# FFN-down of a decoder layer: squares of two token tiles, two k-tiles and two column chunks, 24 of 64 in a seven-product form

## The chip, the core and the metric

One NeuronCore of a Trainium2 chip runs the whole program in one launch. The metric is the device time of one execution in microseconds (us), lower is better; before the change it is 1213.66 us, the median of three runs (1212.97, 1213.66, 1217.4).

## The reference, cut to what matters

One decoder layer over 256 tokens of width 2048, in float32: a token mixer, then the MLP (the part that changes), then a gated per-layer embedding and a final norm.

```python
h2 = rms_norm(x, mlp_norm[i])
x = x + jnp.square(jax.nn.relu(h2 @ w_ffn_up[i])) @ w_ffn_down[i]   # 2048 -> 8192 -> 2048

gate = jax.nn.sigmoid(rms_norm(x, ple_norm[i]) @ w_ple_gate[i])     # 2048 -> 2048
x = x + gate * (p[i] @ w_ple_proj[i])                               # 256 -> 2048
```

## The kernel before

**Split operands.** TensorE multiplies in fp32r, a shortened float32. To keep float32 accuracy every operand is stored twice: h is the value rounded to fp32r, l is the rest (value minus h). Each product is then three matmuls into one PSUM bank: `a_h w_h`, `a_h w_l`, `a_l w_h` (lines 174 to 176). Weights come from HBM as panels of 256 rows by 512 columns, in SBUF a tile of 128 x 1024 float32 (two k-tiles side by side, 512 KB). `load_raw` (L141) issues the DMA from SP's queue, `split_w` (L146) makes `wh` by two 512-wide copies on ScalarE (ACT, L152) and `wl` by one 1024-wide subtraction on VectorE (DVE, L153). The three tiles raw, wh and wl each rotate over 3 buffers (pool `wp`). A buffer is written again only when its last reader is through.

**MLP.** The hidden width of 8192 is worked in two halves (`ffn_half`, L1068). In each, 8 calls of `gemm_wide` (L990) compute 512 hidden columns each; after every half of a call `square` (L1074) squares the positive part of two k-tiles of hidden activations (128 hidden columns by 256 tokens each) and splits them with `split_sb` (L156) into a tile y, which stays in SBUF as the stationary operand of FFN-down. Then `gemm_toks` (L195) runs FFN-down for four chunks n of 512 output columns. For each chunk it goes through 16 panels, each with two k-tiles and two token tiles, and accumulates into two of four PSUM banks (tag mm): 16 x 2 x 2 x 3 = 192 matmuls of 128 x 512 a chunk, 768 a half, 1536 in all. At a chunk's end `scaled_residual` (L1097) adds the two banks to the residual stream x (tiles xr) on VectorE. In the second half, `h3_part` (L1018) follows each chunk: 8 transposes of x on TensorE into a wide PSUM bank (pool psw, two of two banks), copied out by ScalarE (L1031) and VectorE (L1032). They are the operand of the gate product.

**After the MLP.** The projection of p (four short `gemm_toks`, tile pp), then the gate product in chunks: chunks 0 to 2 by `gemm_toks`, chunk 3 from weights that `keep` (L1057) had split earlier into tiles gk: four during the last chunk of FFN-down (hooks at panels 5, 8, 11, 14), two in each of the first two gate chunks. The last chunk is computed token tile by token tile, so that the end of the program is short.

**What sets the order.** Inside the program a scheduler orders the instructions of each engine; weights' splits and some residual additions carry a high priority. Each engine works through its own queue in order, and an instruction that waits holds back all behind it. Up to the end of the token mixer TensorE's order is the written one (L306).

## Time and profile before

| what | value |
|---|---|
| runs | 1212.97, 1213.66, 1217.4 us (median 1213.66) |
| profiled execution | span 1216.2 us; the profile gives no time outside the span, and the span stands 2.5 us above the median and inside the range of the runs |
| TensorE (PE), busy | 1198.4 us, 99% of the span |
| weight loads (PEld), busy | 1028.3 us, 85% |
| VectorE (DVE), busy | 742.8 us, 61% |
| ScalarE (ACT), busy | 640.1 us, 53% |
| DMA | 216.88 MB, mean 178 GB/s |
| granted TensorE clock, mean | 0.996 |

How to read it: a group's row gives the line, the engine, the operation, the tiles written and read (buffer numbers left out), shapes and count, then the busy time in us and the mean duration of one in ns, then the idle time of that engine just before and what ended it. A row of a timeline gives the start, the duration, and the instruction; the distance between two starts need not be the duration of the first, since an engine can begin an instruction before the one ahead has ended. A row of stretches gives the stretch, its length and for each engine the busy time and the number of instructions, then the granted clock, the share of the DMA engines and GB/s. DMA rows give the time from issue to landing.

### The profile page before, as it was taken

How to read it: one execution, taken by the hardware profiler on the slowest of the kernel's cores; microseconds unless marked ns; L12 is line 12 of the kernel's file. 1: busy time of each engine (PE TensorE's matmuls, PEld its weight loads, DVE VectorE, ACT ScalarE, POOL GpSimd, SP SyncE). 2: the span in 40 equal slices, each digit the busy share in tenths (PEclk: the TensorE clock that was granted, in tenths of full speed). 3: DMA queues.
4: the chain of work that ended last, by engine and by line, in shares of the span. 5: the costliest groups of instructions: out<-in, count | busy, mean ns of one | idle time of the engine just before them, and what ended most of it. 6: DMA issues, size and time to landing. Idle time of an engine off the chain costs nothing.

```text
span 1216.2 us, 18355 instructions
## 1 busy us (share of the span) xinstructions
PE 1198.4 (99%) x7142; PEld 1028.3 (85%) x7142; DVE 742.8 (61%) x938; ACT 640.1 (53%) x1175; POOL 15.4 (1%) x65
## 2 busy tenths in 40 slices
...
GB/s 272 124 198 116 168 152 102 108 185 139 133 238 177 180 188 182 187 189 188 193 190 192 192 197 193 182 187 190 188 182 187 192 187 190 193 255 224 200 123 70
DMA packets 60616, 216.88 MB, mean 178 GB/s; under 512 B 6769, under 2 KB 7537, under 8 KB 60145
## 3 DMA queue, kind: packets, MB, share of 16 engines
...
q10 hardware_dynamic: 288, 0.51, 0.1%
...
HBM read 213.59 MB, written 2.10 MB: 177 GB/s over the span
## 4 chain that ended last, share of the span: by engine, by line
PE 93%; DVE 3%; DMA 1%; ACT 1%; issue 1%; ACTq 0%; DVEq 0%
PE u_w L1004 20%; PE u_w L1008 10%; PE d_b L174 9%; PE d_b L175 9%; PE d_b L176 9%; PE gt_b L175 2%; PE gt_b L176 2%; PE gt_b L174 2%; PE wag_b L335 1%; PE zp_b L174 1%; PE zv_b L165 1%; PE zp_b L176 1%; PE zp_b L175 1%; PE zv_b L166 1%; PE zv_b L167 1%; PE o_b L174 1%
## 5 line engine op out<-in xcount | busy, mean ns | idle before, releaser
L1004 PE MATMUL u_w<-h,wh_u 128*128 128x512 f32 x1024 | 362.1, 399 | 0.0
L1008 PE MATMUL u_w<-h,wl_u 128*128 128x256 f32 x1024 | 287.8, 281 | 0.0
L153 DVE TENSOR_TENSOR wl_d<-raw_d,wh_d 128x1024 fp32r<-128x1024 f32 x128 | 156.9, 1225 | 166.8 <-ACT wh_d L152 166.8
L153 DVE TENSOR_TENSOR wl_u<-raw_u,wh_u 128x1024 fp32r<-128x1024 f32 x128 | 156.8, 1225 | 142.2 <-ACT wh_u L152 142.2
L152 ACT ACTIVATE wh_d<-raw_d 128x512 fp32r<-128x512 f32 x256 | 147.5, 624 | 182.0 <-PE d_b L176 161.0
L152 ACT ACTIVATE wh_u<-raw_u 128x512 fp32r<-128x512 f32 x256 | 147.6, 624 | 179.6 <-PE u_w L1004 89.6
L1004 PEld LDWEIGHTS u_w<-h,wh_u 128*128 128x128 f32 x1024 | 192.5, 188 | 47.9
L176 PE MATMUL d_b<-wh_d,y 128*128 128x512 f32 x512 | 199.8, 390 | 0.0
L174 PE MATMUL d_b<-wh_d,y 128*128 128x512 f32 x512 | 199.7, 390 | 0.0
L175 PE MATMUL d_b<-wl_d,y 128*128 128x512 f32 x512 | 199.6, 390 | 0.0
L1008 PEld LDWEIGHTS u_w<-h,wl_u 128*128 128x128 f32 x1024 | 193.7, 189 | 0.0
L176 PEld LDWEIGHTS d_b<-wh_d,y 128*128 128x128 f32 x512 | 96.1, 188 | 19.9
L174 PEld LDWEIGHTS d_b<-wh_d,y 128*128 128x128 f32 x512 | 96.2, 188 | 19.9
L175 PEld LDWEIGHTS d_b<-wl_d,y 128*128 128x128 f32 x512 | 96.2, 188 | 19.6
L153 DVE TENSOR_TENSOR wl_gt<-raw_gt,wh_gt 128x1024 fp32r<-128x1024 f32 x24 | 29.4, 1224 | 24.4 <-ACT wh_gt L152 24.4
L152 ACT ACTIVATE wh_gt<-raw_gt 128x512 fp32r<-128x512 f32 x48 | 27.7, 625 | 23.3 <-PE gt_b L176 19.3
L165 PE MATMUL zv_b<-hTh,wh_zv 128*128 128x256 f32 x128 | 37.7, 294 | 0.0
L165 PE MATMUL zr_b<-hTh,wh_zr 128*128 128x256 f32 x128 | 37.5, 293 | 0.0
L174 PE MATMUL gt_b<-wh_gt,h 128*128 128x512 f32 x96 | 37.4, 389 | 0.0
L175 PE MATMUL gt_b<-wl_gt,h 128*128 128x512 f32 x96 | 37.4, 389 | 0.0
L176 PE MATMUL gt_b<-wh_gt,h 128*128 128x512 f32 x96 | 37.4, 389 | 0.0
L167 PE MATMUL zr_b<-hTh,wl_zr 128*128 128x256 f32 x128 | 37.1, 290 | 0.1
...
## 6 DMA issues: line engine op xcount, KB each, us to landing
raw_u<-in_w_ffn_up_dram SPq DMA_DIRECT2D x128, 512.0 KB, 3.5
raw_d<-in_w_ffn_down_dram SPq DMA_DIRECT2D x128, 512.0 KB, 3.5
...
```

Source lines behind the costliest of these rows:

```text
L152: nc.scalar.activation(wh[:, a * 512 : (a + 1) * 512], raw[:, a * 512 : (a + 1) * 512], AF.Copy)
L153: nc.vector.tensor_tensor(wl, raw, wh.bitcast(F32), op=ALU.subtract)
L165: nc.tensor.matmul(o, w_h, ah, start=first and ct % 2 == 0, stop=False, skip_group_check=True)
L166: nc.tensor.matmul(o, w_h, al, start=False, stop=False, skip_group_check=True)
L167: nc.tensor.matmul(o, w_l, ah, start=False, stop=last, skip_group_check=True)
L174: nc.tensor.matmul(o, a_h, wh[:, 0:n], start=first, stop=False)
L175: nc.tensor.matmul(o, a_h, wl[:, 0:n], start=False, stop=False)
L176: nc.tensor.matmul(o, a_l, wh[:, 0:n], start=False, stop=last)
L335: nc.tensor.matmul(wag_banks[tt][:, 0:288], xg[k // 4][:, k % 4, tt * 128 : (tt + 1) * 128], wr[k], start=k == 0, stop=k == NK - 1,)
L1004: nc.tensor.matmul(bank[:, ct, :].rearrange("p (s t) -> p s t", s=2), wh[:, c], hl, start=k == 0, stop=False, skip_group_check=True,)
L1008: nc.tensor.matmul(bank[:, ct, 0:T], wl[:, c], hl[:, 0, :], start=False, stop=k == 15, skip_group_check=True)
```

## The change

Two chunks of columns are worked together. A `sweep` covers one pair of chunks in one half: 16 squares i, each of two token tiles by two k-tiles by two chunks, hence 8 block products. 10 of the 16 squares (plain) do them as before, 24 matmuls, into four PSUM banks p2, p3, p4 and d22. Squares 2, 4, 7, 9, 11 and 13 (`SEVEN`) use Strassen's form in Winograd's variant: seven products of sums of blocks, 21 matmuls, into p1, p6, p5 and p7 (the two wide banks) and p2, p3 and p4. After square 13 the wide banks are added up on VectorE and into the four blocks of x; after square 15 the other four banks follow. There are four sweeps.

For a seven-product square the activations' sums are made once per half, in `square_seven`: four VectorE operations 128 wide, then seven blocks are split in three pieces instead of one. The weights' sums are made in every sweep by `weights_seven`: two raw panels, four 512-wide VectorE differences (tiles t, float32), their splits th and tl (1024 wide, two tiles each, both used up by one square), and the splits w7h and w7l of three plain blocks.

Around it: raw, wh and wl rotate over 4 buffers instead of 3 once the MLP's pool is open (`ring`); constants of the token mixer move to a pool `mc` that closes with it; the h3 transposes stand behind the projections of p instead of behind the chunks of FFN-down; `keep` is called three, three and two times in gate chunks 0, 1 and 2, loads through `load_raw`, and stores in other tiles; scratch tiles change names (junk and t, ph and u).

```diff
+    mc = rctx.enter_context(tc.tile_pool(name="mc", bufs=1))
...
+    extra = []
+    turns = {"raw": 0, "wh": 0, "wl": 0}
+
+    def ring(tag, dt, name):
+
+        if extra:
+            turns[tag] += 1
+            if turns[tag] % 4 == 0:
+                return extra[0].tile([128, 1024], dt, tag=f"{tag}x", name=name)
+        return wp.tile([128, 1024], dt, tag=tag, name=name)
+
     def load_raw(src, n, name):
-        raw = wp.tile([128, 1024], F32, tag="raw", name=f"raw_{name}")
+        raw = ring("raw", F32, f"raw_{name}")
         nc.sync.dma_start(raw[:, 0:n], src)
         return raw
 
     def split_w(raw, name):
 
-        wh = wp.tile([128, 1024], F32R, tag="wh", name=f"wh_{name}")
-        wl = wp.tile([128, 1024], F32R, tag="wl", name=f"wl_{name}")
+        wh, wl = ring("wh", F32R, f"wh_{name}"), ring("wl", F32R, f"wl_{name}")
...
+    extra.append(fp)
...
+    keep_at = ["yd"] * 5 + ["a5", "ys", "th"]
...
+        where = keep_at[kp]
+        raw = load_raw(w_gate[3, kp].rearrange("p a n -> p (a n)"), 1024, f"gk{kp}")
+        if where == "a5":
+            w = a8(5, f"gk{kp}", F32R)
+            wh, wl = w[:, 0:1024], w[:, 1024:2048]
+        else:
+            bufs = {"yd": 10, "ys": 2, "th": 2}[where]
+            wh, wl = (fp.tile([128, 1024], F32R, tag=where, bufs=bufs, name=f"gk{kp}{c}") for c in "hl")
...
+    SEVEN = (2, 4, 7, 9, 11, 13)
+    F_A11, F_A12, F_A22, F_S1, F_S3, F_S2, F_S4 = range(7)
+    def mm(o, l, r, first, last):
+        nc.tensor.matmul(o, l, r, start=first, stop=last, skip_group_check=True)
+    def mm3(o, a, w, first, last):
+        (a_h, a_l), (w_h, w_l) = a, w
+        mm(o, a_h, w_h, first, False)
+        mm(o, a_h, w_l, False, False)
+        mm(o, a_l, w_h, False, last)
+    def square_plain(src, pr):
+        d = fp.tile([128, 1024], F32R, tag="yd", bufs=10, name=f"yd{pr}")
+        split_sb(d[:, 0:512], d[:, 512:1024], src)
+        def block(i, j):
+            o = j * T + i * 128
+            return d[:, o : o + 128], d[:, 512 + o : 512 + o + 128]
+        return block
+    def square_seven(src, pr, q):
+        if q < 4:
+            y = a8((0, 1, 2, 5)[q], f"ys{pr}", F32R)[:, 0:1792]
+        else:
+            y = fp.tile([128, 1792], F32R, tag="ys", bufs=2, name=f"ys{pr}")
+        yh, yl = (y[:, c : c + 896].rearrange("p (f t) -> p f t", t=128) for c in (0, 896))
+        k1t0, k1t1, k2t0, k2t1 = (src[:, c * 128 : (c + 1) * 128] for c in range(4))
+        sf = fp.tile([128, 4, 128], F32, tag="u", bufs=3, name=f"sf{pr}")
+        nc.vector.tensor_tensor(sf[:, 0], k1t1, k2t1, op=ALU.add)
+        nc.vector.tensor_tensor(sf[:, 1], k1t0, k1t1, op=ALU.subtract)
+        nc.vector.tensor_tensor(sf[:, 2], sf[:, 0], k1t0, op=ALU.subtract)
+        nc.vector.tensor_tensor(sf[:, 3], k2t0, sf[:, 2], op=ALU.subtract)
+        tok0 = src.rearrange("p (k t) -> p k t", k=2)[:, :, 0:128]
+        split_sb(yh[:, 0:2], yl[:, 0:2], tok0)
+        split_sb(yh[:, 2], yl[:, 2], k2t1)
+        split_sb(yh[:, 3:7], yl[:, 3:7], sf)
+        return lambda f: (yh[:, f], yl[:, f])
+    def weights_seven(ra, rb, name):
+        b11, b21, b12, b22 = ra[:, 0:512], ra[:, 512:1024], rb[:, 0:512], rb[:, 512:1024]
+        t = [fp.tile([128, 1024], F32, tag="t", bufs=2, name=f"t{i}_{name}") for i in range(2)]
+        th = [fp.tile([128, 1024], F32R, tag="th", bufs=2, name=f"th{i}_{name}") for i in range(2)]
+        tl = [fp.tile([128, 1024], F32R, tag="tl", bufs=2, name=f"tl{i}_{name}") for i in range(2)]
+        ha, hb = (ring("wh", F32R, f"w7h{i}_{name}") for i in range(2))
+        la, lb = (ring("wl", F32R, f"w7l{i}_{name}") for i in range(2))
+        with tc.high_priority(20000):
+            nc.scalar.activation(ha, ra, AF.Copy)
+            nc.vector.tensor_tensor(la, ra, ha.bitcast(F32), op=ALU.subtract)
+            nc.vector.tensor_tensor(t[0][:, 0:512], b12, b11, op=ALU.subtract)
+            nc.vector.tensor_tensor(t[0][:, 512:1024], b22, b12, op=ALU.subtract)
+            nc.scalar.activation(hb[:, 512:1024], b22, AF.Copy)
+            nc.vector.tensor_tensor(lb[:, 512:1024], b22, hb[:, 512:1024].bitcast(F32), op=ALU.subtract)
+            nc.scalar.activation(th[0], t[0], AF.Copy)
+            nc.vector.tensor_tensor(t[1][:, 0:512], b22, t[0][:, 0:512], op=ALU.subtract)
+            nc.vector.tensor_tensor(t[1][:, 512:1024], b21, t[1][:, 0:512], op=ALU.subtract)
+            nc.vector.tensor_tensor(tl[0], t[0], th[0].bitcast(F32), op=ALU.subtract)
+            nc.scalar.activation(th[1], t[1], AF.Copy)
+            nc.vector.tensor_tensor(tl[1], t[1], th[1].bitcast(F32), op=ALU.subtract)
...
+        return {
+            "b11": half(ha, la, 0), "b21": half(ha, la, 1), "b22": half(hb, lb, 1),
+            "t1": half(th[0], tl[0], 0), "t3": half(th[0], tl[0], 1),
+            "t2": half(th[1], tl[1], 0), "t4": half(th[1], tl[1], 1),
+        }
+    def sweep(src, acts, np_, name, residual_, hooks=()):
+        hooks = dict(hooks)
+        p2, p3, p4, d22 = (mm_bank(f"{name}_{q}") for q in ("p2", "p3", "p4", "d22"))
+        w1, w2 = wide_bank(f"{name}_w1"), wide_bank(f"{name}_w2")
+        p1, p6, p5, p7 = w1[:, 0], w1[:, 1], w2[:, 0], w2[:, 1]
+        n0, n1 = 2 * np_, 2 * np_ + 1
+        begun = set()
+        last_seven = max(SEVEN)
+        npair = len(acts)
+        def put(which, o, a, w, last):
+            mm3(o, a, w, which not in begun, last)
+            begun.add(which)
+        for i in range(npair):
+            if i in hooks:
+                hooks[i]()
+            ra, rb = (load_raw(src[n, i].rearrange("p a n -> p (a n)"), 1024, f"{name}_{n}_{i}") for n in (n0, n1))
+            if i in SEVEN:
+                w = weights_seven(ra, rb, f"{name}_{i}")
+                a = acts[i]
+                fin = i == last_seven
+                for which, o, f, t, last in (
+                    ("p1", p1, F_A11, "b11", fin), ("p2", p2, F_A12, "b21", False), ("p3", p3, F_S4, "b22", False),
+                    ("p5", p5, F_S1, "t1", fin), ("p7", p7, F_S3, "t3", fin), ("p6", p6, F_S2, "t2", fin),
+                    ("p4", p4, F_A22, "t4", False),
+                ):
+                    put(which, o, a(f), w[t], last)
+                if fin:
+                    u = [fp.tile([128, 512], F32, tag="u", bufs=3, name=f"u{c}_{name}") for c in range(3)]
+                    nc.scalar.activation(u[0], p1, AF.Copy)
+                    nc.vector.tensor_tensor(u[1], p6, u[0], op=ALU.add)
+                    residual_(n0, 0, u[0])
+                    nc.vector.tensor_tensor(u[2], p7, u[1], op=ALU.add)
+                    nc.vector.tensor_tensor(u[1], p5, u[1], op=ALU.add)
+                    residual_(n1, 0, u[1])
+                    residual_(n0, 1, u[2])
+                    nc.vector.tensor_tensor(u[2], p5, u[2], op=ALU.add)
+                    residual_(n1, 1, u[2])
+            else:
+                ws = [split_w(r, f"{name}_{n}_{i}") for n, r in ((n0, ra), (n1, rb))]
+                end = i == npair - 1
+                for which, o, tt, b in (("p2", p2, 0, 0), ("p3", p3, 0, 1), ("p4", p4, 1, 0), ("d22", d22, 1, 1)):
+                    for j in range(2):
+                        put(which, o, acts[i](tt, j), ws[b][j], end and j == 1)
+                    if end:
+                        residual_((n0, n1)[b], tt, o)
+    def scaled_residual(n, tt, src):
+        xs = xr[tt][:, n * 512 : (n + 1) * 512]
+        with tc.high_priority(30000):
+            nc.vector.scalar_tensor_tensor(xs, src, s2[:, tt : tt + 1], xs, op0=ALU.mult, op1=ALU.add)
...
-                split_sb(y[:, bi * 512 : bi * 512 + 512], y[:, 1024 + bi * 512 : 1024 + bi * 512 + 512], r)
+                pr = i * 2 + bi
+                if pr in SEVEN:
+                    acts.append(square_seven(r, f"{hf}_{pr}", SEVEN.index(pr)))
+                else:
+                    acts.append(square_plain(r, f"{hf}_{pr}"))
             gemm_wide(w_up[f], h2, f"u{f}", square)
-            ys.append(y)
             if f == 1:
                 inv_ms()
-        if hf == 1:
-            h3_part, h3 = transposed("h3")
-            h3_box.append(h3)
...
-            run(gemm_toks(w_down[n, hf * 16 : hf * 16 + 16], act, f"d{hf}_{n}", scaled_residual, None, ahead if (hf, n) == (1, 3) else ()))
-            if hf == 1:
-                h3_part("ple_norm", n)
-    ahead = {kp: keep for kp in (5, 8, 11, 14)}
+        for np_ in range(2):
+            sweep(w_down[:, hf * 16 : hf * 16 + 16], acts, np_, f"d{hf}{np_}", scaled_residual)
     ffn_half(0)
     ffn_half(1)
-    h3 = h3_box[0]
+    h3_part, h3 = transposed("h3")
...
+        h3_part("ple_norm", n)
...
-        run(gemm_toks(w_gate[n], h3, f"gt{n}", gated_both(n), None, {kp: keep for kp in ((1, 4) if n < 2 else ())}))
+        run(gemm_toks(w_gate[n], h3, f"gt{n}", gated_both(n), None, {kp: keep for kp in ((1, 3, 5) if n < 2 else (1, 3))}))
```

How the instructions stand. **TensorE, first sweep.** Before, chunk 0 of the first half, the third panel: d_0_b are the two accumulators (5812 and 5813 the token tiles), wh_d and wl_d the panel's halves, y the activations.

```order
L174 MATMUL d_0_b_5812<-wh_d_0_2_5854,y_4406 128x512
L175 MATMUL d_0_b_5812<-wl_d_0_2_5855,y_4406 128x512
L176 MATMUL d_0_b_5812<-wh_d_0_2_5854,y_4406 128x512
L174 MATMUL d_0_b_5813<-wh_d_0_2_5854,y_4406 128x512
L175 MATMUL d_0_b_5813<-wl_d_0_2_5855,y_4406 128x512
L176 MATMUL d_0_b_5813<-wh_d_0_2_5854,y_4406 128x512
```

Now, the end of square 1 (plain, d_d is d22) and the first three products of square 2: w7h and w7l are the split plain blocks, d_w a wide bank (p1), d_p p2 and p3, ys the seven activation blocks.

```order
L1085 MATMUL d_d_5881<-wh_d_1_1_5931,yd_1_4408 128x512
L1085 MATMUL d_w_5882<-w7h_d_2_5970,ys_2_4508 128x512
L1085 MATMUL d_w_5882<-w7l_d_2_5972,ys_2_4508 128x512
L1085 MATMUL d_w_5882<-w7h_d_2_5970,ys_2_4508 128x512
L1085 MATMUL d_p_5878<-w7h_d_2_5970,ys_2_4508 128x512
L1085 MATMUL d_p_5878<-w7l_d_2_5972,ys_2_4508 128x512
L1085 MATMUL d_p_5878<-w7h_d_2_5970,ys_2_4508 128x512
L1085 MATMUL d_p_5879<-w7h_d_2_5971,ys_2_4508 128x512
L1085 MATMUL d_p_5879<-w7l_d_2_5973,ys_2_4508 128x512
L1085 MATMUL d_p_5879<-w7h_d_2_5971,ys_2_4508 128x512
```

Four accumulators in place of two change every three or six matmuls, and a square of 24 becomes one of 21; products 4 to 7, on th and tl, follow these.

**VectorE, the same half.** Before, the splits of chunk 0's panels stand one after another, with one square() between them:

```order
L153 TENSOR_TENSOR wl_d_0_2_5855<-raw_d_0_2_5852,wh_d_0_2_5854 128x1024
L1078 TENSOR_TENSOR r_1_5806<-u_w_5713,r_1_5806 128x512
L1079 SCALAR_TENSOR_TENSOR r_1_5806<-r_1_5806 128x512
L153 TENSOR_TENSOR wl_d_0_3_5874<-raw_d_0_3_5871,wh_d_0_3_5873 128x1024
L158 TENSOR_TENSOR y_5613<-r_1_5806,y_5613 128x512
L153 TENSOR_TENSOR wl_d_0_4_5893<-raw_d_0_4_5890,wh_d_0_4_5892 128x1024
```

Now, from the plain square 8 to the plain square 10, with seven-product square 9 and one instruction of square 11 (t is the float32 difference, tl its low part, w7l the low part of a plain block; the two numbers behind d name chunk and square, a single one the square):

```order
L164 TENSOR_TENSOR wl_d_0_8_6220<-raw_d_0_8_6215,wh_d_0_8_6219 128x1024
L164 TENSOR_TENSOR wl_d_1_8_6225<-raw_d_1_8_6217,wh_d_1_8_6224 128x1024
L1134 TENSOR_TENSOR t_d_9_6257<-raw_d_1_9_6255,raw_d_0_9_6253 128x512
L1133 TENSOR_TENSOR w7l_d_9_6265<-raw_d_0_9_6253,w7h_d_9_6263 128x1024
L1135 TENSOR_TENSOR t_d_9_6257<-raw_d_1_9_6255 128x512
L1137 TENSOR_TENSOR w7l_d_9_6266<-raw_d_1_9_6255,w7h_d_9_6264 128x512
L1139 TENSOR_TENSOR t_d_9_6258<-raw_d_1_9_6255,t_d_9_6257 128x512
L1141 TENSOR_TENSOR tl_d_9_6261<-t_d_9_6257,th_d_9_6259 128x1024
L1140 TENSOR_TENSOR t_d_9_6258<-raw_d_0_9_6253,t_d_9_6258 128x512
L1143 TENSOR_TENSOR tl_d_9_6262<-t_d_9_6258,th_d_9_6260 128x1024
L1135 TENSOR_TENSOR t_d_11_6342<-raw_d_1_11_6340 128x512
L164 TENSOR_TENSOR wl_d_0_10_6305<-raw_d_0_10_6300,wh_d_0_10_6304 128x1024
```

Two 1024-wide subtractions for a plain square, eight instructions for a seven-product square; the first difference of square 11, which needs only one of its panels, stands ahead of the splits of square 10.

**TensorE, behind FFN-down.** Before, the transposes stand inside the next chunk of FFN-down (here behind chunk 0 of the second half; x_3158 and x_3159 are the token tiles of x):

```order
L174 MATMUL d_1_b_8962<-wh_d_1_0_8966,y_7044 128x512
L175 MATMUL d_1_b_8962<-wl_d_1_0_8967,y_7044 128x512
L176 MATMUL d_1_b_8962<-wh_d_1_0_8966,y_7044 128x512
L1025 MATMUL h3t<-ident,x_3158 128x128
L174 MATMUL d_1_b_8963<-wh_d_1_0_8966,y_7044 128x512
L175 MATMUL d_1_b_8963<-wl_d_1_0_8967,y_7044 128x512
L1025 MATMUL h3t<-ident,x_3159 128x128
L1025 MATMUL h3t<-ident,x_3158 128x128
L1025 MATMUL h3t<-ident,x_3159 128x128
L176 MATMUL d_1_b_8963<-wh_d_1_0_8966,y_7044 128x512
```

Now, from the last projection of p to the first gate products (pp_b and gt_b are accumulators, wh_gt gate weights, h the transposed operand):

```order
L185 MATMUL pp_b_10398<-wh_pp_0_10401,ph 128x512
L186 MATMUL pp_b_10398<-wl_pp_0_10402,ph 128x512
L187 MATMUL pp_b_10398<-wh_pp_0_10401,pl 128x512
L185 MATMUL gt_b_10457<-wh_gt_0_10461,h_10268 128x512
L186 MATMUL gt_b_10457<-wl_gt_0_10462,h_10268 128x512
L1037 MATMUL h3t<-ident,x_3161 128x128
L1037 MATMUL h3t<-ident,x_3162 128x128
L1037 MATMUL h3t<-ident,x_3161 128x128
L1037 MATMUL h3t<-ident,x_3162 128x128
L187 MATMUL gt_b_10457<-wh_gt_0_10461,h_10268 128x512
L1037 MATMUL h3t<-ident,x_3161 128x128
```

The first three groups of four stand behind projections 0 to 2, the other five lie among the first gate products.

50 lines of the change are left out of this document (19 added, 31 removed).

## Prediction

> **What bounds the kernel now.** I read the page's busy shares first, then the groups of FFN-down, then TensorE's waits, then single matmuls in order of time.
>
> ```profile
> PE 1198.4 (99%) x7142; PEld 1028.3 (85%) x7142; DVE 742.8 (61%) x938; ACT 640.1 (53%) x1175; POOL 15.4 (1%) x65
> L176 PE MATMUL d_b<-wh_d,y 128*128 128x512 f32 x512 | 199.8, 390 | 0.0
> L174 PE MATMUL d_b<-wh_d,y 128*128 128x512 f32 x512 | 199.7, 390 | 0.0
> L175 PE MATMUL d_b<-wl_d,y 128*128 128x512 f32 x512 | 199.6, 390 | 0.0
> L153 DVE TENSOR_TENSOR wl_d<-raw_d,wh_d 128x1024 fp32r<-128x1024 f32 x128 | 156.9, 1225 | 166.8 <-ACT wh_d L152 166.8
> L152 ACT ACTIVATE wh_d<-raw_d 128x512 fp32r<-128x512 f32 x256 | 147.5, 624 | 182.0 <-PE d_b L176 161.0
> ```
>
> TensorE is busy for 99% of the span, and FFN-down's matmuls never waited (0.0 us idle before them). VectorE waits for ScalarE's copies, and these wait for TensorE to free a weight buffer. TensorE sets the pace; the others follow. All of its waits in the program:
>
> ```profile
> PE wag_b L335 <- DMA wag<-in_w_wag_dram: 7.7, 1, 7.7
> PE rnb L533 <- DVE rnp L158: 0.7, 1, 0.7
> PE h3t L1025 <- DVE x L1100: 0.5, 1, 0.5
> PE h2t L1025 <- DVE x L963: 0.4, 1, 0.4
> ```
>
> What does one matmul cost? Not the 390 ns of its row: matmuls overlap. Single instructions in order of time, then stretches: FFN-up of the first half, FFN-down of the first and second half, projections, gate chunks 0 to 2, end.
>
> ```profile
> 575.42 0.39 PE L175 MATMUL d_b<-wl_d,y 128*128 128x512 f32 x1
> 575.65 0.39 PE L176 MATMUL d_b<-wh_d,y 128*128 128x512 f32 x1
> 575.88 0.39 PE L174 MATMUL d_b<-wh_d,y 128*128 128x512 f32 x1
> ```
>
> ```profile
> 391.00:575.20 184.20, 183.77 (x1042) 159.23 (x1041) 111.32 (x119) 93.80 (x169) 0.00 (x0) 1.00 0.60 186
> 575.20:749.50 174.30, 174.30 (x771) 144.35 (x770) 84.61 (x74) 74.83 (x131) 0.00 (x0) 1.00 0.63 193
> 930.40:1107.50 177.10, 177.10 (x793) 145.74 (x792) 97.07 (x92) 88.73 (x159) 0.00 (x0) 1.00 0.65 208
> 1107.50:1120.10 12.60, 12.08 (x58) 9.66 (x57) 8.76 (x11) 12.06 (x25) 0.00 (x0) 1.00 0.54 181
> 1120.10:1185.40 65.30, 65.30 (x290) 54.09 (x289) 36.02 (x38) 34.10 (x64) 0.00 (x0) 1.00 0.53 164
> 1185.40:1216.20 30.80, 22.51 (x145) 20.43 (x143) 11.78 (x27) 11.20 (x22) 0.00 (x0) 0.90 0.19 69
> ```
>
> Starts lie 0.23 us apart; the first half's FFN-down puts its 768 matmuls into 174.3 us, 0.2267 each. That is the price I use. After a stretch's length come TensorE, weight loads, VectorE and ScalarE, near the end the granted clock and the DMA share.
>
> **The matmuls removed.** 24 squares lose 3 of 24 matmuls each: 72 x 0.2267 = **16.3 us** (by the 390 ns of the rows it would be 28.1, counting overlapped time twice). The remaining ones keep shape and operands, so the price stays. The Trainium skill, "TensorE: Matmul & The Clock Gate", section "Back-to-back issue gap", gives 215.7 ns for an isolated gap at 512 columns, and about 131 ns in a stream with weight loads; the removed matmuls would then be worth 15.5 or 9.4 us. Neither agrees with the stretch: this stream runs at 226.7 ns, and a measured price of the very instructions that go decides.
>
> **The work on the weights that is added.** It hides only if VectorE and ScalarE keep ahead of a faster TensorE. Their prices are again distances between starts, from stretches without idle time: VectorE at 37 us, ScalarE at 1109 us.
>
> ```profile
> 37.17 0.69 DVE L158 TENSOR_TENSOR hTl<-tC_t,hTh 128x512 fp32r<-128x512 f32 x1 [0.35 <-ACT hTh L157]
> 37.78 0.69 DVE L393 TENSOR_TENSOR tD_t<-tD_t,s_bc 128x512 f32<-128x512 f32 x1
> 38.38 1.22 DVE L153 TENSOR_TENSOR wl_zk<-raw_zk,wh_zk 128x1024 fp32r<-128x1024 f32 x1
> 39.52 0.69 DVE L158 TENSOR_TENSOR hTl<-tD_t,hTh 128x512 fp32r<-128x512 f32 x1
> ```
>
> ```profile
> 1109.48 1.06 ACT L261 ACTIVATE junk_n<-x 128x1024 f32<-128x1024 f32 x1
> 1110.45 0.19 ACT L261 ACTIVATION_READ_ACCUMULATOR junk_n<-x 128x1 f32 x1
> ...
> 1111.74 1.15 ACT L152 ACTIVATE wh_pp<-raw_pp 128x512 fp32r<-128x512 f32 x2
> 1112.79 0.47 ACT L1031 ACTIVATE h<-h3t,par_sb 128x256 fp32r<-128x256 f32 x1
> ```
>
> VectorE: 0.60 us for 512 columns, 1.14 for 1024. ScalarE: 0.97 for 1024, 1.05 for two of 512.
> - Seven-product square: VectorE 3 x 1.14 (w7l, tl, tl) + 5 x 0.60 = 6.42 us; ScalarE 3 x 0.97 + 0.53 = 3.44; TensorE 21 x 0.2267 = 4.76.
> - Plain square: VectorE 2 x 1.14 = 2.28; ScalarE 2.10; TensorE 24 x 0.2267 = 5.44.
>
> A seven-product square alone is VectorE's: 6.42 against 4.76. But none follows another directly. Where they are densest (squares 7 to 13) a pair is 8.70 us of VectorE and 5.54 of ScalarE against 10.20 of TensorE. A sweep is 6 x 6.42 + 10 x 2.28 = 61.3, plus 4 additions of 0.60 and 8 residuals of 0.74 (row below) = 69.6 us, against 366 x 0.2267 = 83.0. Before, a half had 64 x 1.14 + 8 x 0.74 = 78.9 us of VectorE's work in 174.3. It goes from 45% to 84%: it fits, without much room.
>
> ```profile
> L1100 DVE SCALAR_TENSOR_TENSOR x<-d_b,s2sq,x 128x512 f32<-128x512 f32 x16 | 11.2, 743 | 0.0
> ```
>
> Does each operand come in time? Four buffers of raw, wh and wl are two squares: VectorE can be one square ahead. I follow squares 7 to 13 in the listed order, with S9's first matmul at 0: S9 to 4.76, P10 to 10.20, S11 to 14.96. The splits of S9 end at -0.4 while its fourth weight sum is read at 4.1: 4.5 us ahead. Then S11's first difference stands before P10's splits, and it needs a raw panel whose buffer S9 frees with its first t[1] difference, at -4.4. So the loop is: freed, loaded, one difference (0.60), P10's two splits (2.28), S11's w7l, difference, w7l, difference (1.14 + 3 x 0.60), freed again: 5.8 us and the load, against 10.20 per pair. Load times of FFN-down's panels, and of gate panels loaded beside them (minimum, median, maximum):
>
> ```profile
> DMA to landing us min/median/max: 3.3/3.5/5.5
> ```
>
> ```profile
> DMA to landing us min/median/max: 4.3/4.8/5.6
> ```
>
> With 3.5 us the loop is 9.3 and VectorE stays ahead; P10's first split is ready at 1.3 and read at 5.0. With 4.8 it is 10.6: 0.4 us lost per pair, on a lead of nearly 3. With 5.5, 11.3: 1.1 lost, on a lead of 2. There are two such turns per sweep (9 to 11 to 13), then plain squares give the lead back. So no wait by this walk. The tiles th and tl, one set for every square, are free when the square before has read them, 8.8 us ahead of their next reading; behind the waiting ScalarE copy stand the copies of the plain square after it, 4 us early.
>
> The unknown: how often a wait slips through all the same. Ends: none, and 0.7 us (the longest wait of a matmul for a VectorE result, above) at each of 24 squares, 16.8 us. Nothing excludes less than none by half a microsecond. The walk stands near the first end; I take one wait of 0.5 per sweep: **+2.0 us**.
>
> **The rest.** TensorE's wait of 0.5 us for x before a transpose goes, since the first transposes now need columns finished a sweep earlier: **-0.5**. The 32 transposes move and cost the same. Their copies now meet the projections and the first gate chunk: ScalarE had 12.06 us of work in 12.60 there, and keeps up only because five of eight groups lie among the gate products (three panels, 8 us, more). If it does not, TensorE waits for h, 0 to 2 us; I take 0, since each gate panel reads just two of the sixteen blocks. The four `keep` splits that leave FFN-down add 4 x 1.14 = 4.6 us of VectorE and 4.2 of ScalarE to a gate stretch that has 36.02 and 34.10 of 65.30: hidden; without that cover 4.6. Their panels raise gate chunk 0 and 1 from 10 to 11 loads. `square_seven` adds at most 6 x 0.60 = 3.6 us per square to VectorE, 21.6 a half, beside FFN-up, where it has 111.32 of 184.20: hidden. Banks: p1, p5, p6 and p7 are added up during squares 14 and 15 (10.9 us for 7.7 of VectorE's work, splits apart); d22's residual has the next sweep's first 18 matmuls, 4.1 us. Pool `mc`, scratch names and the fourth buffer cost nothing: the order ahead of the MLP is the same, and no matmul waited there for a buffer.
>
> **Sum.** -16.3 + 2.0 - 0.5 = -14.8. The profiled execution's span would go from 1216.2 to 1201.4; that span is 2.5 above the median, to which I apply the difference: 1213.7 - 14.8 = **1198.9 us**.
>
> **Rivals.**
> - *The panel loop binds.* Two 512 KB loads at once take longer than 5.6 us (DMA share goes from 0.63 toward 0.7), the lead of 2 to 4 us is gone by square 11, and TensorE waits 1 to 3 us a sweep at squares 11 to 13, or at the sweep's start. For it: VectorE at 84%, in-order queues. Against: 319 GB/s were moved in the program's first 22 us (below). With 4 to 10 us lost: 1201 to 1208.
>
> ```profile
> 0.00:22.00 22.00, 14.30 (x55) 11.09 (x55) 15.04 (x29) 11.24 (x23) 8.04 (x49) 1.00 0.85 319
> ```
>
> - *Slower: VectorE sets the pace in the sweeps.* Place: the pairs of squares 7 to 13. If it also waits for ScalarE before each of six subtractions instead of working ahead (3 x 0.97 + 0.53 + 2 x 1.05 = 5.5 us), a pair takes 14.2, 4.0 more than TensorE. 24 x 4.0 less 1.06 at each of 16 spare plain squares is 79 us: 1213.7 - 16.3 + 79 = 1276. It decides from 0.68 us of waiting per seven-product square (16.3 / 24) on. Against: the order lets differences stand between the waits.
> - *Slower: the clock.* Eight accumulators change every three or six matmuls; if each change made TensorE pause, the granted clock could fall, as in the program's end (0.90 in the last stretch). Over four sweeps of 83 us that is 332 / 0.9 - 332 = +36.9: 1213.7 - 16.3 + 36.9 = 1234. Against: before, two accumulators alternated every three matmuls at a clock of 1.00. The Trainium skill, "TensorE: Matmul & The Clock Gate", section "A second HAM failure mode: psum-queue depth-cycling", tells of cycling through banks with short pauses that let the clock swing; by that rule this change is at risk, and the trace of FFN-down does not show it.
> - *Better than the forecast*: something waits less than before by over 4 us: below 1195.
>
> That the matmuls do not go is excluded: the listed order has 72 fewer.
>
> **How the numbers follow.** Forecast with no or small waits (1195 to 1201): 0.62. Panel loop: 0.24, a fifth of it above 1207.6. VectorE's pace: 0.05. Clock: 0.02. Better: 0.05. Waits of about the whole gain: 0.02. About 0.5%, 6.1 us, is what a measurement of this kernel can tell from no change. Faster: 0.62 + 0.05 + 0.24 x 0.8 = 0.86; same: 0.05 + 0.02 = 0.07; slower: 0.07. The range takes the forecast, half a microsecond of gain and the runs' spread below (1194), and the panel loop above (1208).
>
> **What would show it.** FFN-down's stretches at 166 us a half and 0.2267 us a matmul; seven-product groups with no idle time before them; VectorE near 84% there, its longest wait for ScalarE or for a panel, TensorE's list of waits as short as above. Wrong: TensorE waiting for th, tl or wl by over 0.7 us a square, a matmul dearer than 0.23 us, or a granted clock below 1.00 in the sweeps.

## The result and the profile after

| what | value |
|---|---|
| the changed kernel | 1204.61 us, median of 4 runs (1203.33 to 1205.96) |
| the kernel before, beside it | 1213.66 us, median of 4 runs (1212.97, 1213.66, 1213.67, 1217.4) |
| ratio | 0.9918, 95% interval 0.9900 to 0.9936 |
| profiled execution of after | 1204.86 us, span 1203.1 us (before: span 1216.2) |

The change is worth about 9 us here, and 12 us in the second comparison below. The forecast of 1198.9 us was 5.7 us too low, and the result lies inside its range.

The first lines are from the page of after: busy shares, and the largest group of FFN-down's matmuls, which all stand on one line of the program now.

```profile
PE 1183.2 (98%) x7070; PEld 1015.0 (84%) x7070; DVE 872.9 (73%) x1186; ACT 674.7 (56%) x1203; POOL 15.5 (1%) x65
L1085 PE MATMUL d_p<-wh_d,yd 128*128 128x512 f32 x480 | 154.5, 389 | 0.8 <-ACT wh_d L163 0.8
```

72 matmuls have gone and TensorE is busy 15.2 us less; VectorE has 130.1 us more. Next, stretches of after: FFN-up of the first half, FFN-down of the first and second half, projections, gate chunks 0 to 2.

```profile
393.90:575.50 181.60, 181.60 (x1031) 157.71 (x1032) 117.39 (x153) 95.96 (x180) 0.00 (x0) 1.00 0.59 186
575.50:741.56 166.06, 166.06 (x734) 137.51 (x733) 141.15 (x161) 89.90 (x132) 0.00 (x0) 1.00 0.63 199
922.45:1090.30 167.85, 166.75 (x734) 137.00 (x733) 140.21 (x160) 90.00 (x133) 0.00 (x0) 1.00 0.61 200
1090.30:1104.60 14.30, 13.00 (x61) 10.14 (x62) 10.43 (x15) 13.74 (x30) 0.00 (x0) 1.00 0.78 249
1104.60:1172.30 67.70, 67.70 (x309) 55.91 (x308) 46.47 (x54) 43.32 (x85) 0.00 (x0) 1.00 0.63 202
```

FFN-down of the first half takes 166.06 us where it took 174.30; its 732 matmuls cost 0.2269 us each. VectorE is busy 85% of that time, and the granted clock is 1.00. In the second half 1.1 us without TensorE's work stand in the stretch. Projections and gate chunks grew from 77.90 to 82.00 us: 24 of the 32 transposes moved there, and that is about 3 us of the 4.1 (the second half's FFN-down took 177.10 us before, the first half's 174.30; from first matmul to first matmul 177.29 and 174.09). The rest is waits. The waits of TensorE in after (the ones that are not in before's list are the second, the third, and the two for pp_b):

```profile
PE wag_b L346 <- DMA wag<-in_w_wag_dram: 8.0, 1, 8.0
PE h3t L1037 <- DVE h L1044: 0.8, 1, 0.8
PE d_p L1085 <- ACT wh_d L163: 0.8, 1, 0.8
PE rnb L544 <- DVE rnp L169: 0.7, 1, 0.7
PE pp_b L187 <- DVE pl L169: 0.5, 1, 0.5
PE h2t L1037 <- DVE x L974: 0.4, 1, 0.4
PE pp_b L185 <- DVE x L1206: 0.3, 1, 0.3
```

The matmul d_p that waited starts at 1006.69 us and is the first of the fourth sweep; the others are the first and the third matmul of the projections, and the third group of transposes, at 1101.31. None is inside the dense part of a sweep (squares 7 to 13). VectorE's longest waits on FFN-down's tiles, in the same view:

```profile
DVE t_d L1134 <- DMA raw_d<-in_w_ffn_down_dram: 22.0, 16, 3.2
DVE tl_d L1143 <- ACT th_d L1142: 19.6, 16, 1.6
DVE wl_d L164 <- ACT wh_d L163: 13.9, 16, 1.6
```

### The profile page after: what moved, and what is told of

Same layout as the page of the kernel before. It is cut to its first block, busy times and chain, and to the rows that moved or that the text cites. A ratio compares the mean times of both kernels' runs of the same rounds, so it can differ in the third digit from the quotient of the medians.

```text
span 1203.1 us, 18401 instructions
## 1 busy us (share of the span) xinstructions
PE 1183.2 (98%) x7070; PEld 1015.0 (84%) x7070; DVE 872.9 (73%) x1186; ACT 674.7 (56%) x1203; POOL 15.5 (1%) x65
## 4 chain that ended last, share of the span: by engine, by line
PE 89%; DVE 6%; DMA 2%; ACT 2%; issue 1%; ACTq 0%; DVEq 0%
PE u_w L1016 20%; PE d_p L1085 15%; PE u_w L1020 10%; PE d_w L1085 4%; PE d_d L1085 4%; DMA raw_d<-in_w_ffn_down_dram 2%; PE gt_b L187 2%; PE gt_b L186 2%; PE gt_b L185 2%; PE wag_b L346 1%; PE zp_b L185 1%; PE zv_b L176 1%; PE zp_b L187 1%; PE zp_b L186 1%; PE o_b L186 1%; PE o_b L185 1%
## 5 line engine op out<-in xcount | busy, mean ns | idle before, releaser
L1085 PE MATMUL d_p<-wh_d,yd 128*128 128x512 f32 x480 | 154.5, 389 | 0.8 <-ACT wh_d L163 0.8
L163 ACT ACTIVATE wh_d<-raw_d 128x512 fp32r<-128x512 f32 x160 | 89.1, 620 | 36.8 <-issue 18.5
L1085 PEld LDWEIGHTS d_p<-wh_d,yd 128*128 128x128 f32 x480 | 90.1, 188 | 20.0 <-ACT wh_d L163 1.2
L164 DVE TENSOR_TENSOR wl_d<-raw_d,wh_d 128x1024 fp32r<-128x1024 f32 x80 | 95.4, 1220 | 14.3 <-ACT wh_d L163 13.9
L1085 PE MATMUL d_p<-wl_d,yd 128*128 128x512 f32 x240 | 93.6, 390 | 0.0
L1085 PE MATMUL d_d<-wh_d,yd 128*128 128x512 f32 x160 | 55.8, 389 | 0.0
L1085 PEld LDWEIGHTS d_p<-wl_d,yd 128*128 128x128 f32 x240 | 45.1, 188 | 9.7 <-DVE wl_d L164 0.6
L1138 ACT ACTIVATE th_d<-t_d 128x1024 fp32r<-128x1024 f32 x24 | 25.4, 1058 | 47.6 <-DVE t_d L1135 30.2
L1085 PE MATMUL d_w<-th_d,ys 128*128 128x512 f32 x144 | 48.2, 389 | 0.0
L1142 ACT ACTIVATE th_d<-t_d 128x1024 fp32r<-128x1024 f32 x24 | 25.4, 1059 | 35.4 <-DVE t_d L1140 31.2
L1143 DVE TENSOR_TENSOR tl_d<-t_d,th_d 128x1024 fp32r<-128x1024 f32 x24 | 29.4, 1225 | 19.9 <-ACT th_d L1142 19.6
```

The source lines that it names most:

```text
L163: nc.scalar.activation(wh[:, a * 512 : (a + 1) * 512], raw[:, a * 512 : (a + 1) * 512], AF.Copy)
L164: nc.vector.tensor_tensor(wl, raw, wh.bitcast(F32), op=ALU.subtract)
L1085: nc.tensor.matmul(o, l, r, start=first, stop=last, skip_group_check=True)
L1138: nc.scalar.activation(th[0], t[0], AF.Copy)
L1143: nc.vector.tensor_tensor(tl[1], t[1], th[1].bitcast(F32), op=ALU.subtract)
```

## The experiments

Each kernel was timed beside the kernel before; the ratios are to it.

**Both kernels again.** No edit.

> The kernel before, unchanged. Theory A (the profiled execution of before was a long one): its span is about 3 to 4 us shorter than 1216.2, and the stretch that is shorter lies outside FFN-down, FFN-up and the gate, which keep 174.3, 181, 177 and 78 us. Theory B (the span of before is always 1216, and the change's kernel gains 13 in spans and only 9 in times because something outside the span grew): the span is 1216 again, with a time near 1213.7.

> The changed kernel, unchanged, beside the kernel before on one chip. Theory A: the ratio stays near 0.992, span 1202 to 1204, first-half sweeps 166 us. Theory B: the ratio moves by over 0.002 between two sessions, and the stretches in FFN-down move with it.

Before: 1216.74 us (12 runs), ratio 0.9996 (0.9983 to 1.0008). After: 1204.71 us, ratio 0.9899 (0.9886 to 0.9912), 12.2 us faster than the 1216.87 us of before in this comparison. Why 9 us first and 12 now? The runs of before form two groups: 8 of 26 between 1212.99 and 1214.51, 18 between 1216.21 and 1217.9 (of the 12 runs of before_again one, 1214.92, stands between the groups). Three of the four runs of the first comparison were of the lower group. The profiled execution of before_again (span 1212.0) is of the lower group too, that of before (span 1216.2) of the upper. The stretch of FFN-up of the first half in each, before_again first:

```profile
393.10:571.50 178.40, 178.40 (x1033) 157.36 (x1034) 109.33 (x117) 92.95 (x168) 0.00 (x0) 1.00 0.60 189
```

```profile
393.50:575.20 181.70, 181.70 (x1033) 157.81 (x1034) 109.33 (x117) 92.87 (x168) 0.00 (x0) 1.00 0.60 186
```

The same instructions, no wait, clock 1.00, and 3.3 us apart: 0.348 or 0.355 us for each of 512 pairs of a 512- and a 256-column matmul. So theory A was right that the profiled execution was a long one, and wrong about where: the 3.3 us lie in FFN-up. All profiled executions of the changed kernel and its variants show the slower pace there (181.60 above). So before runs one stretch, which the change does not touch, faster in some of its executions: 8 of 26 here, 1 of 17 in the next comparison, 2 of 13 in the one after, 3 of 10 in the last. Of the changed kernels only single runs may be of that kind (one of seven_earlier, 1201.34 us, stands 4.5 below the next). What sets the pace is not known. In after_again's profile TensorE loses 3.1 us to waits as in after, but partly at other places: none at the start of the fourth sweep, more at the projections, and 0.4 inside the dense part of that sweep.

**No seven-product squares.** The reorganisation stays, with 16 tiles yd.

```diff
-    SEVEN = (2, 4, 7, 9, 11, 13)
+    SEVEN = ()
```

> The changed kernel with no seven-product square: all 64 squares plain, in the same sweeps, everything else as changed. Theory of the prediction (a removed matmul is worth its 0.2267 us and the seven-product squares cost TensorE next to nothing): 15.5 to 16.5 us slower than the changed kernel, so 3 to 7 us slower than before, a sweep pair of 174.1 us a half. Rival (the seven-product squares cost part of their gain in waits): only 9 to 12 us slower than the changed kernel and level with before.

1216.64 us, ratio 1.0001 (0.9992 to 1.0010). No wait of TensorE is left from the sweeps on. From the first sweep to the projections, the second FFN-up among it, plain_sweeps and then after:

```profile
574.80:1104.00 529.20, 529.20 (x2563) 445.20 (x2562) 277.14 (x258) 240.35 (x422) 0.00 (x0) 1.00 0.61 191
```

```profile
575.50:1090.30 514.80, 513.70 (x2490) 431.30 (x2489) 398.35 (x468) 271.86 (x435) 0.00 (x0) 1.00 0.62 196
```

The sweeps, the moved transposes and the fourth buffers are together worth nothing that can be measured. The whole gain is the seven-product form: 14.4 us in this stretch, of the 16.3 that its missing matmuls cost. Behind it after takes 112.8 us to the end and plain_sweeps 110.8, so 2 us of it are lost again; by the times the gain is 11.9 us, as the rival had it.

**How much room VectorE has.** The last subtraction of a seven-product square is done again, with the same result: once more (one_more, 1.14 us per square, 27.4 us in the program), or twice more (two_more, `range(3)`).

```diff
-            nc.vector.tensor_tensor(tl[1], t[1], th[1].bitcast(F32), op=ALU.subtract)
+            for _ in range(2):
+                nc.vector.tensor_tensor(tl[1], t[1], th[1].bitcast(F32), op=ALU.subtract)
```

> In each seven-product square the last weight split on VectorE is done three times, 2 x 1.14 us more of VectorE's work in each of 24 squares; a pair of squares is then 10.98 us of VectorE against 10.20 of TensorE. Theory of the prediction (VectorE hides with a lead of 2 to 4 us): the four spare plain squares refill the lead, waits of TensorE grow by 0 to 3 us in all. Rival (VectorE already sets the pace in places): TensorE waits for most of the added 2.28 us at most of the squares, 25 to 50 us more.

> The last weight split of each seven-product square is done twice, 1.14 us more of VectorE's work in each of 24 squares: a sweep is 69.6 + 6.8 = 76.4 us of VectorE against 83.0 of TensorE. With two more it was 83.3, a full VectorE, and 15.4 us slower. Theory E (VectorE's work is free up to the length of the sweep, and what is over falls on TensorE): 0 to 3 us slower than the changed kernel. Rival (each microsecond on VectorE costs its share from the start, since waits of in-order engines add up): half of the 15.4, 6 to 9 us slower.

two_more: 1220.1 us, ratio 1.0036 (1.0022 to 1.0049). one_more: 1216.79 us, ratio 0.9999 (0.9990 to 1.0008), so one subtraction more costs 12 us, the whole gain, although VectorE's work of a sweep (69.6 + 6 x 1.14 = 76.4 us) is still below TensorE's 83.0. That is more than either theory expected. two_more, 15.4 us above after, lies between its two theories. TensorE's waits in one_more:

```profile
PE d_w L1085 <- DVE tl_d L1144: 7.7, 9, 1.5
PE pp_b L185 <- DVE x L1207: 2.4, 1, 2.4
PE d_p L1085 <- DVE wl_d L164: 1.9, 2, 1.3
```

The room of VectorE is not what its busy share says; what uses it up is found after the next three edits.

**Three small edits that did not help.** ring3_up opens the fourth buffers only around the sweeps, seven_earlier moves the seven-product squares, pl_first splits p ahead of the second half.

```diff
-    extra.append(fp)
...
+        extra.append(fp)
         for np_ in range(2):
             sweep(w_down[:, hf * 16 : hf * 16 + 16], acts, np_, f"d{hf}{np_}", scaled_residual)
+        extra.clear()
```

> The changed kernel with raw, wh and wl in 3 buffers everywhere but in the sweeps, where there are 4. FFN-up of the first half ran at 11.31 us per half call in every profile of the changed kernel, and at 11.31 or 11.09 in two profiles of before. Theory C (the fourth buffer settles FFN-up at the slow pace): with 3 buffers some runs show a first half of FFN-up of 178.4 us in place of 181.7, and the times spread over two groups 3 to 4 us apart. Rival (the pace is not a matter of the buffers): one group near 1204.7, or nothing but the waits at the change of rings, 0 to 2 us more.

1210.81 us (1208.47 to 1213.89), ratio 0.9947 (0.9935 to 0.9958): 6 us slower than after, which neither theory expected. Its profiled execution has FFN-up at the slow pace (181.8 us), with three buffers as before: nothing here shows that the fourth buffer sets it. Without it the gate chunks take 74.8 us instead of 67.8 in the profiled execution, which is the slowest of the six runs, and TensorE waits there:

```profile
PE gt_b L186 <- DVE wl_gt L164: 4.2, 5, 1.3
```

```diff
-    SEVEN = (2, 4, 7, 9, 11, 13)
+    SEVEN = (2, 4, 6, 8, 10, 12)
```

> Seven-product squares at 2, 4, 6, 8, 10, 12 in place of 2, 4, 7, 9, 11, 13: five turns of the panel loop in a row, and three plain squares behind the last. Theory D (TensorE loses its 3 us where a sweep ends, since VectorE comes out of square 13 with its additions and residuals late): the waits at the start of the fourth sweep and of the projections (1.2 and 1.1 us) go, 1 to 2.5 us faster than the changed kernel. Rival (the panel loop binds in the dense run of squares): TensorE waits at squares 8 to 12, 2 to 8 us slower than the changed kernel.

1206.05 us, ratio 0.9902 (0.9887 to 0.9916): no change against after. The waits at the start of a sweep and of the projections went, and four others came. All four stand in plain squares of the dense run (the matmuls that waited start at 623.59, 634.53, 982.26 and 1066.38 us), which is where the rival put them, though they are smaller than it said:

```profile
PE d_p L1085 <- DVE wl_d L164: 1.8, 4, 0.7
PE h3t L1037 <- DVE h L1044: 1.6, 1, 1.6
```

```diff
     ffn_half(0)
+    praw = load_raw(pT.rearrange("p a t -> p (a t)"), 512, "pT")
+    ph, pl = (fp.tile([128, 512], F32R, tag="p", bufs=2, name=nm) for nm in ("ph", "pl"))
+    split_sb(ph, pl, praw[:, 0:512])
     ffn_half(1)
     h3_part, h3 = transposed("h3")
 
-    praw = load_raw(pT.rearrange("p a t -> p (a t)"), 512, "pT")
-    ph, pl = (fp.tile([128, 512], F32R, tag="u", bufs=3, name=nm) for nm in ("ph", "pl"))
-    split_sb(ph, pl, praw[:, 0:512])
```

> The split of p (ph and pl) is done ahead of the second half's FFN-up, in tiles of its own. Theory D: TensorE's wait of 0.6 us for pl goes and the residuals of p2 to d22 come 0.6 us earlier on VectorE: 0.5 to 1.2 us faster than the changed kernel. Rival (the next wait takes its place): the first projections then wait as long for the residuals or for h, no difference beyond 0.3 us.

1204.13 us, ratio 0.9890 (0.9878 to 0.9903): no change. The wait for pl went, and the waits for x and h beside it grew:

```profile
PE h3t L1037 <- DVE h L1044: 1.6, 1, 1.6
PE pp_b L185 <- DVE x L1206: 0.9, 1, 0.9
PE d_p L1085 <- DVE x L1206: 0.6, 1, 0.6
```

seven_earlier and pl_first moved a small delay to another place. So I looked for where VectorE's time goes. Its timeline in after, from the last subtraction of square 9 to that of square 11, one pair of squares:

```profile
622.04 1.23 DVE L1143 TENSOR_TENSOR tl_d<-t_d,th_d 128x1024 fp32r<-128x1024 f32 x1 [1.19 <-ACT th_d L1142]
623.18 0.68 DVE L1135 TENSOR_TENSOR t_d<-raw_d 128x512 f32<-128x512 f32 x1
623.79 2.35 DVE L164 TENSOR_TENSOR wl_d<-raw_d,wh_d 128x1024 fp32r<-128x1024 f32 x2
626.44 1.22 DVE L1133 TENSOR_TENSOR w7l_d<-raw_d,w7h_d 128x1024 fp32r<-128x1024 f32 x1 [0.30 <-ACT w7h_d L1132]
...
629.48 1.23 DVE L1141 TENSOR_TENSOR tl_d<-t_d,th_d 128x1024 fp32r<-128x1024 f32 x1
630.62 0.68 DVE L1140 TENSOR_TENSOR t_d<-raw_d,t_d 128x512 f32<-128x512 f32 x1
632.51 1.23 DVE L1143 TENSOR_TENSOR tl_d<-t_d,th_d 128x1024 fp32r<-128x1024 f32 x1 [1.21 <-ACT th_d L1142]
```

From 622.04 to 632.51 are 10.47 us, and from there to the same subtraction of square 13 (642.54) 10.03: on average 10.25 us a pair, where TensorE takes 10.20 (the eight such turns of the four sweeps take 10.03 to 10.91, on average 10.36). 8.70 of it is work, 1.2 is the wait of tl[1] for th[1]: the order puts tl[1] right behind the difference that th[1] is made from (L1140), and ScalarE needs its 0.97 us in between. VectorE's loop is full with the wait counted in. On average it runs no faster than TensorE, so whatever is added comes out of TensorE's time. In one_more the wait is still there, and the turn is longer by the added work; tl[1] of squares 9, 11 and 13:

```profile
623.56 1.23 DVE L1144 TENSOR_TENSOR tl_d<-t_d,th_d 128x1024 fp32r<-128x1024 f32 x1 [1.19 <-ACT th_d L1142]
634.78 1.22 DVE L1144 TENSOR_TENSOR tl_d<-t_d,th_d 128x1024 fp32r<-128x1024 f32 x1 [1.21 <-ACT th_d L1142]
645.91 1.23 DVE L1144 TENSOR_TENSOR tl_d<-t_d,th_d 128x1024 fp32r<-128x1024 f32 x1 [1.13 <-ACT th_d L1142]
```

These turns take 11.22 and 11.13 us, 1 us more than TensorE's 10.20. Seven of the eight are like that and the last takes 13.0; together they stand 9.6 us over TensorE's pace, most of the 12. It also shows why two_more, with twice the added work, lost only 3.3 us more. There the scheduler put other work in front of most tl[1]: they waited 4 times for th[1], 3.5 us in all, where one_more's waited 16 times, 18.2 us.

**The order on VectorE, alone.** The differences of t[1] get a higher priority; tl[0] then stands behind them, and covers the time in which ScalarE makes th[1].

```diff
+            with tc.high_priority(2000):
-            nc.vector.tensor_tensor(t[1][:, 0:512], b22, t[0][:, 0:512], op=ALU.subtract)
-            nc.vector.tensor_tensor(t[1][:, 512:1024], b21, t[1][:, 0:512], op=ALU.subtract)
+                nc.vector.tensor_tensor(t[1][:, 0:512], b22, t[0][:, 0:512], op=ALU.subtract)
+                nc.vector.tensor_tensor(t[1][:, 512:1024], b21, t[1][:, 0:512], op=ALU.subtract)
```

> Only the order on VectorE changes: the two differences of t[1] get a higher priority, so the subtraction tl[0] stands behind them and not between them, and ScalarE can make th[1] while VectorE makes tl[0]. In the changed kernel every dense seven-product square has VectorE waiting 1.19 to 1.21 us for th[1] ahead of tl[1] (19.6 us in the program). Theory F (the loop is full): a pair of squares is 8.70 us of VectorE's work, 1.2 of that wait and about 0.4 for a panel, 10.3 in all against TensorE's 10.20, so the lead cannot be refilled; with the wait gone (below 8 us in the program) it can, and TensorE's waits in the sweeps shrink from 1.2 us and those around the projections may too: ratio to before 0.986 to 0.990, 1201 to 1205 us in a comparison in which the changed kernel stood at 1204.7. Rival G (the panels set the loop): VectorE then waits as much longer for raw panels and TensorE's waits stay: ratio 0.990, the same as the changed kernel.

1200.46 us (1200.09 to 1201.62), ratio 0.9867 (0.9854 to 0.9881), 4.2 us below after in its second comparison; theory F had a ratio of 0.986 to 0.990. In the profiled executions, from first matmul to first matmul, 1.9 us of it lie in the second half's sweeps (165.98 for 167.86) and 0.9 in the projections (13.38 for 14.27); 1.4 lie ahead of FFN-up, where the two kernels are alike. So 2.8 us are the order's, as far as one execution of each can tell. VectorE at the same place in th_first; the last two subtractions of square 9, then of square 11:

```profile
617.95 1.22 DVE L1142 TENSOR_TENSOR tl_d<-t_d,th_d 128x1024 fp32r<-128x1024 f32 x1
619.09 1.22 DVE L1144 TENSOR_TENSOR tl_d<-t_d,th_d 128x1024 fp32r<-128x1024 f32 x1
...
628.36 1.23 DVE L1142 TENSOR_TENSOR tl_d<-t_d,th_d 128x1024 fp32r<-128x1024 f32 x1 [0.61 <-ACT th_d L1138]
629.50 1.22 DVE L1144 TENSOR_TENSOR tl_d<-t_d,th_d 128x1024 fp32r<-128x1024 f32 x1
```

No wait for th[1] is left (6.0 us for th[0] in the program), and from the sweeps on TensorE's list of waits holds only h3t:

```profile
PE h3t L1037 <- DVE h L1044: 0.9, 1, 0.9
```

The turn itself is no shorter than in after: 10.41 us (619.09 to 629.50), and 10.36 on average over the eight turns. What fills it has changed. These are VectorE's longest wait on FFN-down's tiles in th_first, one copy that it waits for, and TensorE's last matmul with the first panel of square 10:

```profile
DVE wl_d L164 <- ACT wh_d L163: 26.7, 30, 2.2
630.26 1.15 ACT L163 ACTIVATE wh_d<-raw_d 128x512 fp32r<-128x512 f32 x2 [0.98 <-ACT th_d L1143]
629.78 0.39 PE L1085 MATMUL d_p<-wh_d,yd 128*128 128x512 f32 x1
```

By the order of the four buffers, square 12's first wh is written over square 10's. ScalarE's copy starts 0.09 us after the matmul's end (629.78 + 0.39 = 630.17), the next one, at 631.62, 0.09 us after the end of the square's last matmul (631.14 + 0.39). So here VectorE waits because it is as far ahead as the buffers let it be. Such a wait can give way to added work, as the next run shows. The one for th[1] does not (19.6 us in after, 18.2 in one_more): it hangs on VectorE's own result.

The lead can be read off. TensorE reads the low half of t[1] of square 9 at these starts, in after and then in th_first:

```profile
626.19 0.39 PE L1085 MATMUL d_w<-tl_d,ys 128*128 128x512 f32 x1
```

```profile
624.79 0.39 PE L1085 MATMUL d_w<-tl_d,ys 128*128 128x512 f32 x1
```

It was ready at 622.04 + 1.23 = 623.27 in after, 2.9 us ahead, and at 619.09 + 1.22 = 620.31 in th_first, 4.5 us ahead.

**The same order with the added subtraction.** th_first and the second subtraction of one_more.

> The order of th_first and the added second subtraction tl[1] of one_more (1.14 us more of VectorE's work per seven-product square, 27.4 us in the program; the values do not change). Theory F: the 1.2 us that the order frees per square pay for it: a loss of 0 to 3 us against th_first instead of the 12 us that it cost in the changed kernel's order; 1203 to 1208 us, TensorE's waits for tl below 2 us. Rival G (the panels set the loop, or the loss came from the work itself): 8 to 12 us, 1212 to 1217 us, TensorE's waits for tl 5 us or more.

1203.58 us (1203.13 to 1203.76), ratio 0.9891 (0.9875 to 0.9906): 3.1 us above th_first, where the same 27.4 us of work cost 12 in after's order. TensorE waits for no tl, and VectorE's wait for wh_d went from 26.7 to 6.4 us: that was the room. So the amount of VectorE's work had not used up the room; the order had, with the wait for th[1] in the loop. That it was not the loading of panels rests on the traces: at squares 11 and 13 of after VectorE waits at most 0.5 us for a panel or its copy, and its waits for panels fell from 22.0 to 14.4 us in th_first, where rival G had them grow. The new order also reads the raw panels earlier and so lets them go earlier; no run separates that part.

**A difference on GpSimd**, in after's order.

```diff
-            nc.vector.tensor_tensor(t[0][:, 512:1024], b22, b12, op=ALU.subtract)
+            nc.gpsimd.tensor_tensor(t[0][:, 512:1024], b22, b12, op=ALU.subtract)
```

> One of the four weight differences of each seven-product square (512 columns, second half of t[0]) is made on GpSimd instead of VectorE: 0.60 us less of VectorE's work per square, 14.4 us in the program. No run so far shows such an operation on GpSimd. Theory F: if GpSimd's result comes before VectorE would have needed it (it stands beside a chain of three others), TensorE's waits in the sweeps go, ratio to before 0.987 to 0.990; th[0] waits for it instead. If it takes over 2 us, th[0] and so tl[0] come late by the rest, and with 1 us late per square TensorE loses up to 10 us: ratio 0.998. Rival G: no change, ratio 0.990.

1213.94 us, ratio 0.9981 (0.9969 to 0.9992). VectorE is relieved by 14.4 us, and the kernel loses 9 us. The group on GpSimd, and TensorE's longest waits in the sweeps:

```profile
L1135 POOL TENSOR_TENSOR t_d<-raw_d 128x512 f32<-128x512 f32 x24 | 43.5, 1811 | 876.3 <-DMA raw_d<-in_w_ffn_down_dram 422.0 <-ACT wh_d L163 419.5 <-DVE x L1206 25.3
```

```profile
PE d_p L1085 <- DVE wl_d L164: 5.2, 6, 1.4
```

It takes 1.81 us instead of 0.60, and the chain behind it frees the panel later: VectorE's wait for panels is 30.2 us, in after 22.0. That this is how the 9 us come about is argued, not shown.

**Seven squares instead of six**, on th_first.

```diff
-    SEVEN = (2, 4, 7, 9, 11, 13)
+    SEVEN = (1, 3, 5, 7, 9, 11, 13)
```

> The order of th_first, and seven squares in place of six in each sweep: 1, 3, 5, 7, 9, 11 and 13, so 28 of 64 in the seven-product form (one more tile ys, one less yd). 12 more matmuls go: 12 x 0.2267 = 2.7 us. VectorE's work of a sweep goes from 69.6 to 73.8 us, TensorE's from 83.0 to 82.3. Theory F with the loop freed: th_first_more showed that 76.4 us of VectorE's work per sweep cost 2.8 us in the program, so 73.8 costs 0 to 1: 1197.5 to 1199 us where th_first had 1200.5, ratio 0.984 to 0.986. Rival H (the sweep's end): from square 14 over the sum of the wide banks to square 1 of the next sweep VectorE has 21.6 us of work in 21.1 of TensorE's, and it comes there with a backlog: TensorE waits 0.5 to 1.5 us a sweep at squares 1 and 3, 1200 to 1204 us, ratio 0.986 to 0.990.

1203.76 us (1203.01 to 1205.18), ratio 0.9904 (0.9886 to 0.9922). Neither theory: the sweeps did what the first said, and the loss is at the end of the program. From the first sweep to the projections, th_first and then seven_sevens:

```profile
574.20:1087.00 512.80, 512.80 (x2490) 431.68 (x2489) 401.65 (x470) 275.37 (x438) 0.00 (x0) 1.00 0.60 198
```

```profile
574.30:1084.40 510.10, 510.10 (x2478) 429.50 (x2477) 414.61 (x495) 278.73 (x437) 0.00 (x0) 1.00 0.62 199
```

2.7 us less, as expected, and no wait. The last two stretches (gate chunks 0 to 2, end), th_first and then seven_sevens:

```profile
1100.40:1168.20 67.80, 67.80 (x309) 55.87 (x308) 46.45 (x54) 43.30 (x85) 0.00 (x0) 1.00 0.62 202
1168.20:1199.00 30.80, 22.56 (x145) 20.47 (x143) 11.77 (x27) 11.31 (x22) 0.00 (x0) 0.91 0.19 69
```

```profile
1098.30:1168.50 70.20, 68.73 (x309) 55.65 (x308) 45.56 (x53) 43.59 (x85) 0.00 (x0) 1.00 0.59 195
1168.50:1201.30 32.80, 22.79 (x145) 20.53 (x143) 12.82 (x28) 13.68 (x24) 0.00 (x0) 0.88 0.18 64
```

4.4 us more, and 0.5 in the projections. The scheduler ordered the end anew: gt3b now begins at 1174.20 us, when half of gt3a is done, and gt3a's last matmul starts at 1184.44; in th_first gt3b follows the last matmul of gt3a at 1179.09. The two token tiles' last work is no longer staggered. Of the 2.4 us lost in the gate chunks, 1.5 show as TensorE's waits for wl_gt. An order that holds the end fixed was not tried; by the stretches it would stand near 1200.5 - 2.7 = 1197.8 us, which is an estimate.

## Why the prediction was right, and where not

- **The price of the matmuls: right.** 0.2267 us was used, 0.2269 measured, with eight accumulators and new operands. (The quotient given for it, 174.3 / 768, is 0.2270; from first matmul to first matmul the first half takes 174.09 us before and 165.93 after, 0.2267 in both.) The Trainium skill, "TensorE: Matmul & The Clock Gate", section "Back-to-back issue gap", gives about 216 ns for an isolated gap at 512 columns and about 131 ns in a stream with weight loads. The trace again lies above both, at 226.7 ns.
- **"I take one wait of 0.5 per sweep", and 0 for the transposes' copies: too small, in the right bounds.** From start to start, TensorE lost 3.0 us at four places, none in the dense part: the start of the fourth sweep (1.0), the projections (0.5 and 0.6) and h3t (1.0). The last was forecast as 0 to 2 and taken as 0. The other three make the 2.0 of the forecast, but that is luck: it saw them at the seven-product squares, one a sweep. The wait for x before a transpose that was to go (-0.5) went.
- **The sum against its own execution: -14.8 forecast, 1203.1 - 1216.2 = -13.1 us measured in the span.** The h3t wait is 1.0 of the 1.7 us between them; the rest is spread over several stretches, 0.4 of it ahead of FFN-up.
- **The step that cost most: "that span is 2.5 above the median, to which I apply the difference".** The profiled time of after is 1.76 us above its span, so before's profiled execution was, by estimate, one near 1218 us, of the upper group, and the sum was made from it; the median of 1213.66 was of the lower. A span also has to be raised by that 1.76 before it is compared with times: set beside them as it was, 1216.2 seemed to lie inside the range of the runs. 1218.0 - 14.8 is 1203.2, 1.7 us from the 1204.86 of after's profile. The three runs shown (1212.97, 1213.66, 1217.4) held the two groups already.
- **"Does each operand come in time?": the walk's conclusion held, its margin did not.** It let VectorE work without a stop and had square 9's splits end 0.4 us before the square's first matmul, 4.5 us ahead of the reading of the fourth weight sum. They ended 0.7 us after it (623.27 against 622.56), 3.4 us ahead of that reading at 626.64. The missing piece is the wait for th[1], 1.2 us at squares 4, 9, 11 and 13 of every sweep. one_more shows what it means: a loop without margin. The walk counted on 1.5 us to spare in every pair (10.20 - 8.70), and there was none.
- **The rivals.** *The panel loop binds*: VectorE's wait for panels came (22.0 us), and so did the wait at a sweep's start, but at squares 11 and 13, where the lead should have gone, panels cost VectorE at most 0.5 us and th[1] 1.2. The time lies in that rival's span of 1201 to 1208, not in the forecast's own of 1195 to 1201, and for another reason. *VectorE sets the pace* names the right mechanism, a wait for ScalarE in front of subtractions, and overrates it: tl[1] waited 16 times in 24 squares, w7l twice, tl[0] never, and the plain squares' wl 16 times in 80. *The clock*: 1.00 in every stretch of the sweeps. The Trainium skill, "TensorE: Matmul & The Clock Gate", section "A second HAM failure mode: psum-queue depth-cycling", tells of a clock that swings where TensorE pauses briefly between groups while it cycles through banks. In after's sweeps eight accumulators change every three to six matmuls, TensorE is without work for 1.1 us in all, and the clock stays at 1.00.
